# A decoder trunk on one core: operands of products begin at multiples of 128 bytes, and the written order of the pieces changes with it

## The chip, the core and the metric

The kernel runs on one core of a Trainium2 chip. TensorE (PE in the rows) multiplies, VectorE (DVE), ScalarE (ACT) and GpSimd (POOL) work on tiles, SyncE (SP) issues the transfers. Operands lie in SBUF, 128 partitions side by side; products come out in PSUM, in 8 banks of 512 float32 columns. The metric is the device time of one execution in microseconds (us); less is better.

## The reference, cut to what matters

256 tokens of width 1024 go through two layers in float32. Layer 0 is a recurrent block with a gated FFN, layer 1 an attention block of three branches with a gated FFN:

```
u = rmsnorm(h); z = u @ w_in                      # 1024 -> 2048
y = gelu(z[:1024]); x = causal_conv(z[1024:])     # 4 taps
r, i = sigmoid(per-head products of x)            # 8 heads of 128
h += (y * scan(a(r), b(r, i, x))) @ w_out
h += (silu(g) * up) @ w_out2                      # g, up = u @ w_in2, hidden 2816
k, v of three branches = rmsnorm(h) @ kv_w        # compressed, selected, window
h += (gated sum of 3 softmax attentions, 16 heads of 64, 4 key groups) @ w_o
h += (silu(g) * up) @ w_out2                      # hidden 2816
```

## The kernel before, in words

Every large product is made of three on TensorE: both operands are split into a high part (a copy rounded to the type fp32r) and a low part (the rest), and `mm3` adds high x high, high x low and low x high into the same PSUM bank (lines 340 to 342; `z_mm` does the same on line 411).

**The stream of weights.** `Weights` brings 192 weight tiles, in the order of `STREAM`, from memory into a ring of 4 `raw` tiles on SP's queue. `pieces` splits each: the first piece copies it to a `wh` tile (ACT, lines 137 or 144), the second subtracts to a `wl` tile (DVE or POOL, lines 193 and 198); there are 6 of each. Tiles in `WHOLE` (the weights of the compression) are multiplied as they lie in `raw`, so the ring's place is free only when TensorE has read them. All these tiles have `WT` columns.

**Four stages.** Stage A, the recurrent block: 16 products `z` of 24 matmuls of 256 columns, the convolution and gates and a scan (`lru`), then 96 matmuls of 512 columns in `a_proj` (`accf0o`). FFN 0 and FFN 1 (`ffn`): 11 chunks of 256 hidden columns; in chunks 1 to 10 `in_fm` has four weight tiles of 24 matmuls each (stationary: 128 columns of `wh` or `wl`; moving: 256 columns of the activation `u`), then `out_both` has two tiles of 12 matmuls (stationary: 128 columns of the hidden activation `fhh`, `fhl`; moving: 512 columns of `wh` or `wl`). Stage B, the attention: `kc_mm`, `q_mm` and `v_mm` (key, query and value products), `cm_mm` (the compression, 60 columns, straight from `raw`), `scores`, `tr_p`, `pv_mm`, `o_mm`.

**What sets the order.** In stages A and B the order of every engine is written by hand as the tables `PLAN_A` and `PLAN`: `play` runs one piece of a generator for each word (`z12` a product, `w14` a split's first or second piece, `l2` a piece of the scan, `cm02` a compression product); a letter behind it picks an engine (A, V, G) or a bank (a, m, t). In the FFNs, program order and free buffers set it.

**Where operands begin.** A tile of 1072 float32 columns has 4288 bytes a partition, 33.5 times 128, so of the 16 tiles raw, wh and wl, which lie behind each other, every second begins 64 bytes past a multiple of 128. The addresses in the built program, modulo 128, of the operands that this text speaks of:

| operand | before | after |
|---|---|---|
| raw, wh, wl | 64 and 0 in turn | 0 |
| activations u (moving in z and in_fm) | 64 | 0 |
| fhh, fhl in FFN 0 / in FFN 1 (stationary in out_both) | 96 / 64 | 0 / 0 |
| yh, yl (stationary in a_proj) | 32 | 0 |
| qT, kh, kl, vh, vl, identr, negr | 64 | 0 |
| msk (the identity of transposes), gw, zero | 32 | 0 |

By these addresses, before: product z1 has wh and wl at 0, z2 both at 64. In FFN 0, the four tiles of a chunk's `in_fm` have (wh, wl) at (0, 64), (64, 64), (64, 0), (0, 0); in FFN 1 at (64, 64), (0, 0), (0, 64), (64, 64). In the first half of the `out_both` of FFN 0 that begins at 190.69 us the moving wh and wl begin at 64, in its second half at 0.

Of the kernel before, what the change touches and what calls it, by code (L numbers as in the profile page):

```python
# [57 lines left out]
PLAN_A = """  # L58
na0aV na0 na1 na0 na0 na1 na1 nt0 na1t e0 nt0 w0 w0G e0 nt0 nt0 nt0 nt0 nt1a nt1m nt1 nt1a nt1t nt1 w1 w1 w2 w3 w2V z0
c0 d0 d0 d0 c0 d0 d0 d0 c0 d0 c0 w3G z1 d0G d0 d0 d0 d0 c1 c1 c1 c1 d0 d0 d0 z2 d0 d0 d0 w4 w4 g0 g0 g1 g1 g1 c2 d0 d0  # L60
g0 d0 c2 d0 d0 d0 c2 c2 w5 d0 d0 d0 d0 z3 c3 d0 d0 c3 d0 g2 g2 g2 d0 d0 c3 d0 d0 d0 c3 w6 w6 z4 g3 g3 w7 g3 c4 d0 d0
d0 c4 w5G d0 d0 d0 c4 d0 d0 d0 c4 w7 z5 g4 g4 g4 c5 d0 d0 d0 c5 c5 d0 d0 d0 d0 l0 l1 w8 w8G z6 d0 d0 c5 g5 g5 g5 d0 d0
d0 c6 c6 c6A d0 d0 d0 d0 l2t d0 c6 w9 z7 c7 w9a g6 g6 g6 d0 d0 d0 c7 d0 d0 d0 d0 d0 c7 d0 d0 w10 w11 w11G c7 l0 w10 z8
l1 g7 g7mA w12 w13 g7m l0V l0V l1 l3t l1 l1 l2a l0 z9 y0A z10 l2 l3a l3 w12G l2 y0V l3 w13G l2 l3 y1 y1V w14 y0 y0
w14a y2 y2V y1 y1 w15 w15 z11 y3 y2 y3V w16a w16 y2 z12 z13 y4 y4V y3 y3 y5 y5V w17 w17 z14 y4 y4 w18 w18 z15 y6 y6V
y5 y5 w19 gf0 w20 w19 y7 y7 o00 y6 y7 y6 y7 w20 o01 o02 o03 o10 o11 w21 w21 w22 w22 o04 o05 w23 w23 o12 w24 w24 o06
o07 r0 r0 r0 r0 r0 r0 o13 w25 w25 o14 o15 w26 w26 w27 w27V o16 nf0 nf0 nf0 nf0 nf0 nf0 o17 r1 r1 r1 r1 r1 r1a
"""


PLAN = """
w90 w91 w91 w92 hn0 w90 hn0 hn0G hn0 hn0A nt0 hn1 nt0 nt0 nt0 hn1 w92G kc00 kc01 nt0 nt0 hn1 w93V hn1 hn1 kc02 w93 nt1
nt1 w94V nt1 kc03 nt1 w94 kc10 nt1V kc04 w95V nt1 kc11 w95 kc12 w96V w97 w96 kc05 kc06 w97 x0 w98V w98 kc07 kc13 kp0
cp0 kp0 kc14 w99V kp0 w99 kc15 w100 ct011 ct011 kc16 ct000V kp0 kc17 ct000V ct010 kp0 ct010 kp0V q00 w100 kp1 w101G
kt00 kp1t kt00 w101 kp1 q01 q02 kt00 kp1 ct001 w102A q03 cp1 ct001 ct101 ct100 w103 w102 ct101 q10 q11 q12t w104A kt01
kp1 w103 w104 ct100 w105 bl0V q04 kt01V q05 bl0aV bl0V q06 bl0 kp1V w105 q07 ct110 qp00 qg0 qp01 qp00 qp00 q13V q14
ct110 q15 w106V qp00 qp00 qp00 qg0 w106 qp00 w107 qp01 qp01 w107 w108 qp01 qp01 qp01V w109 qp01 w108 qp02 qt000 q16
q17 qp10V qp02 qp02 qt000 cm00aA w109G qp02 qp02 w110 qt010 kt01 qp10 qp10 cm01 qt010m qg1 w110 qg1 qg1 w111 ct111
ct111 s000t w111 qp02 qg0G cm02G cm03 qp02 w112 bl1V v00 s000 bl1 s010m s010 qp11 s000 bl1 bl1 w113V qt011a w112 qt011
v01V qp11 qp11 s010 qp10 qp10 qp10 s011t cg0 qp10V kt10 v02 s011 qp12A s001 w113 kt10G qp11 qp11 cg0 w114m w114tG s000  # L80
s000 v10 cg0 v11 s001 s001 s010 v12 kt10 qp12 qp12 cg0 v03 cg0 w115 kt11a s010 s011 s020 w115G w116V v13 co0t qt021a
vp0V cm10m vp0 qt100V qt021V w117 kt11 kt11 co0 qt020m qp11 s020t ck w116G qp12V qp12 qp12V qt020 cm11 cm12 s020 ckA
qt100 s011 gG qp12 w117 ck ck s001 qt121a s001 cm13 vp1 vp1 s020 ck s021m cg1 qp11 ck ck qt120a s021m cg1 s011 t000m
qt120t qt121 s030t cg1 qt111a qt110 t000V cs00a s030V cs01 cs03 t000 s021 cg1 cs02A cg1 cz0t qt110 t010m t010 t001m
s020V s100 cz0V w118 s030 co1a co1V cz0 s100 cz0 cz0 qt111 cv cv s030 t010 s031 s030 cz0 s100 t011m s021 t001V cs10t
s031A cz0 cs12 cs11 t001 cs13 s021 cz0V s101 s100 cz0V s031 s100 t020a pt00m cv cz1 s110t s101 t011 s110 pt00 pt02a
s031G s102t s031 t011 s101 pv00a t020 s101 pt01m s102V t021m s101 t030a pt01 cz1 t031a t020 s102 s102 s103m pt02V s102
pv00V t021 pv01a s110 cz1 s103 cz1 s103 pt03 t021 pv02 s110 s110 pv00 pv01V pv00 s103 s111t cz1V pv00 cz1 s103 pt03
t030 pv01 pv01 s112 s111 t031 pv02 cz1 t030 s111 t100 t101m w118G pv02 s111 t100 t031 pv03a t103aA pv01 t102 cz1V t101
s112 w119a s122 s121m pv02 pv02 t101a s111 cz1 s113m t100 t103t t102 pt10 s112 t102 s120t w119G t103 pt10a pv03V s113V  # L90
pv10t s130 s112 pv03 pv03V pv03 s113 s112 s113 s113V s120 w120 s120 o00G w120 pv10 t110m w121 t113 s121 w121G o01
t110m s121 s120 s120V o02t t110 w122 s122 pt11m t112m pv10 pv10 pt11V t112 pv10 o03 t113 pt12 t112 s121 t111m t111
w122G s121 t113 s130 s131m s122 o04 t111 pt12V s130 s123t s123 s131 s123 pv11 s122 s122 s130 s130 s131 s123 s123V o10
pv11 w123 s131 pv11 pv11V t120 pv11 s131 t122 w123 t123m s132m t120 t120 t123V o11 t122 t122A w124 t121 t121V o12
s133t o05 s132 s132 w124G t123 s133 pt13m o13 s132 s132V w125 w125G s133 t121 pt13V pv12t s133 s133V w126 w127V x1
w127G pv12V t132V pv12 t131m pv12 t130m pv12 o06 t132V t132 t130 t130 w126G t133 t131 t131 o07 t133 t133 on0 on0 o14
pv13 w128V on0 on0 on0 o15 pv13 pv13 pv13 u pv13 w128 w129V u u o16 u u o17 u w129G on1 on1 on1 on1t on1aA
"""
# [1137 lines left out]
```

## Time and profile before

| | us |
|---|---|
| median of 3 runs (lowest to highest) | 649.74 (648.31 to 651.39) |
| profiled execution | 650.03 |
| its span, first to last instruction | 648.1 |
| PE busy | 627.9 |
| DVE busy | 412.0 |
| ACT busy | 325.8 |
| POOL busy | 118.1 |

The profiled execution is 0.3 us above the median, and 1.9 us of it lie outside the span. A matmul's busy time overlaps with the next one's, so what a matmul costs is read from the distance between starts, not from its busy time. [...]

### The profile page before, as it was taken

How to read it: one execution, taken by the hardware profiler on the slowest of the kernel's cores; microseconds unless marked ns; L12 is line 12 of the kernel's file. 1: busy time of each engine (PE TensorE's matmuls, PEld its weight loads, DVE VectorE, ACT ScalarE, POOL GpSimd, SP SyncE). 2: the span in 40 equal slices, each digit the busy share in tenths (PEclk: the TensorE clock that was granted, in tenths of full speed). 3: DMA queues.
4: the chain of work that ended last, by engine and by line, in shares of the span. 5: the costliest groups of instructions: out<-in, count | busy, mean ns of one | idle time of the engine just before them, and what ended most of it. 6: DMA issues, size and time to landing. Idle time of an engine off the chain costs nothing.

```text
span 648.1 us, 10441 instructions
## 1 busy us (share of the span) xinstructions
PE 627.9 (97%) x4067; PEld 560.7 (87%) x4067; DVE 412.0 (64%) x636; ACT 325.8 (50%) x595; POOL 118.1 (18%) x132
## 2 busy tenths in 40 slices
PE   7998899999999999999998999999999999999997
PEld 5898777999999999978998796776899999999996
DVE  5888957665555555469963878988765555555542
ACT  5579645454444444443624467855454444444430
POOL 3215020300000000001453547764100000000000
PEclk8999799999999999999996998999999999999999
DMA  8443654875555655526425140234285565556621
GB/s 294 137 163 131 193 196 135 282 250 196 179 185 190 194 189 183 184 94 206 153 83 192 66 163 1 98 99 130 92 272 191 193 194 173 191 192 192 191 70 66
DMA packets 31380, 106.68 MB, mean 165 GB/s; under 512 B 4014, under 2 KB 5730, under 8 KB 31203
## 3 DMA queue, kind: packets, MB, share of 16 engines
q1 hardware_dynamic: 31331, 106.02, 49.5%
q8 instruction: 32, 0.52, 0.3%
q14 instruction: 17, 0.14, 0.1%
HBM read 104.95 MB, written 1.05 MB: 164 GB/s over the span
## 4 chain that ended last, share of the span: by engine, by line
PE 86%; DVE 7%; ACT 4%; DMA 1%; issue 1%; POOL 0%; SPq 0%; DVEq 0%; ACTq 0%
PE accf L342 6%; PE accf L340 6%; PE accf L341 6%; PE f1u L342 3%; PE f1u L341 3%; PE f1u L340 3%; PE f0g L340 3%; PE f1g L340 3%; PE f0g L342 3%; PE f0g L341 3%; PE f1g L341 3%; PE f0u L341 3%; PE f1g L342 3%; PE f0u L340 3%; PE f0u L342 3%; PE z L411 3%
## 5 line engine op out<-in xcount | busy, mean ns | idle before, releaser
L198 DVE TENSOR_TENSOR wl<-raw,wh 128x1024 fp32r<-128x1024 f32 x147 | 180.1, 1230 | 146.5 <-ACT wh L137 146.3
L137 ACT CAST wh<-raw 128x1024 fp32r<-128x1024 f32 x161 | 167.9, 1049 | 184.5 <-issue 41.8
L342 PE MATMUL accf<-wh,fhl 128*128 128x512 f32 x176 | 69.5, 395 | 0.0
L340 PE MATMUL accf<-wh,fhh 128*128 128x512 f32 x176 | 69.4, 395 | 0.0
L341 PE MATMUL accf<-wl,fhh 128*128 128x512 f32 x176 | 69.2, 393 | 0.0
L198 POOL TENSOR_TENSOR wl<-raw,wh 128x1024 fp32r<-128x1024 f32 x17 | 42.6, 2512 | 46.4 <-ACT wh L137 32.1
L342 PE MATMUL f1u<-uhf,wl 128*128 128x256 f32 x160 | 45.1, 282 | 0.0
L341 PE MATMUL f1u<-ulf,wh 128*128 128x256 f32 x160 | 45.0, 281 | 0.0
L340 PE MATMUL f0g<-uhf,wh 128*128 128x256 f32 x160 | 45.0, 281 | 0.0
L340 PE MATMUL f1u<-uhf,wh 128*128 128x256 f32 x160 | 44.9, 281 | 0.0
L340 PE MATMUL f1g<-uhf,wh 128*128 128x256 f32 x160 | 44.8, 280 | 0.0
L340 PE MATMUL f0u<-uhf,wh 128*128 128x256 f32 x160 | 44.8, 280 | 0.0
L341 PE MATMUL f0u<-ulf,wh 128*128 128x256 f32 x160 | 44.7, 279 | 0.0
L341 PE MATMUL f1g<-ulf,wh 128*128 128x256 f32 x160 | 44.7, 279 | 0.0
L342 PE MATMUL f1g<-uhf,wl 128*128 128x256 f32 x160 | 44.6, 279 | 0.0
L342 PE MATMUL f0g<-uhf,wl 128*128 128x256 f32 x160 | 44.6, 279 | 0.0
L341 PE MATMUL f0g<-ulf,wh 128*128 128x256 f32 x160 | 44.6, 279 | 0.0
L342 PE MATMUL f0u<-uhf,wl 128*128 128x256 f32 x160 | 44.4, 277 | 0.0
L342 PEld LDWEIGHTS accf<-wh,fhl 128*128 128x128 f32 x176 | 33.1, 188 | 7.8
L341 PEld LDWEIGHTS accf<-wl,fhh 128*128 128x128 f32 x176 | 33.1, 188 | 7.0
L340 PEld LDWEIGHTS accf<-wh,fhh 128*128 128x128 f32 x176 | 33.1, 188 | 6.8
L1011 ACT ACTIVATE pr<-s,sm 128x128 f32<-128x128 f32 (+1 forms) x64 | 26.2, 422 | 8.9 <-DVE sm L1003 6.6
(310 smaller groups left out, 1525.9 us busy)
## 6 DMA issues: line engine op xcount, KB each, us to landing
raw<-in_wsrc_dram SPq DMA_DIRECT2D x184, 512.0 KB, 3.7
raw<-in_wsrc_dram SPq DMA_DIRECT2D x8, 536.0 KB, 4.2
hres<-in_x_dram SPq DMA_DIRECT2D x4, 256.0 KB, 3.3
gw<-in_gatew_dram SPq DMA_DIRECT2D x1, 1024.0 KB
gain<-in_gains_dram SPq DMA_DIRECT2D x2, 512.0 KB, 6.5
out_dram<-hres SPq DMA_DIRECT2D x8, 128.0 KB, 1.8
tab<-in_hvec_dram SPq DMA_DIRECT2D x1, 256.0 KB, 4.9
tab<-in_rope_c_dram SPq DMA_DIRECT2D x1, 128.0 KB, 3.8
```

Source lines behind the costliest of these rows:

```text
L137: self.nc.scalar.copy(dst, src)
L198: self.on.pick(nc.gpsimd if i in LOW_ON_POOL else nc.vector).tensor_tensor(lo[:, :w], t[:, :w], f32v(h[:, :w]), ALU.subtract)
L340: T.matmul(ps, ah, bh, start=start, stop=False)
L341: T.matmul(ps, ah, bl, start=False, stop=False)
L342: T.matmul(ps, al, bh, start=False, stop=stop)
L411: T.matmul(zs[i], w[:, k * P:(k + 1) * P], u[:, k, :], start=(n == 0 and k == 0), stop=(n == 2 and k == KT - 1))
L1011: A.activation(pr[:, h1 + i, br], sv[:, br], AF.Exp, bias=sm[:, 0, h0 + i, br:br + 1], accum_out=sm[:, 1, h0 + i, br:br + 1])
```

## The change

`WT` becomes 1088 columns (4352 bytes, 34 times 128), the query tile gets 16 columns of zeros behind the gate columns (so `QC` begins its second and third product at columns 320 and 704; the first is 320 columns wide instead of 304, and 8 transfers are 544 KB instead of 536), small tiles are padded to multiples of 32 columns, and two small tiles of `cmp_k` share the places of two of `cmp_gelu`. Both tables are written anew with the same pieces; here is one row of `PLAN_A` before and after.

```
-    + [1024] * 8 + [1072] * 8 + [1024] * 12 + [1024] * 8
+    + [1024] * 8 + [1088] * 8 + [1024] * 12 + [1024] * 8
...
-WT = 1072
+WT = 1088
...
-l1 g7 g7mA w12 w13 g7m l0V l0V l1 l3t l1 l1 l2a l0 z9 y0A z10 l2 l3a l3 w12G l2 y0V l3 w13G l2 l3 y1 y1V w14 y0 y0
+w11 w11G c7 c7 l0 l1 z8G g7 g7mA w12 w13m w10 g7m w12G l0V l1 l3tA l1 w14 l1 w13V l0V l0G l2a l3a l3m z9 y1m y1V y1 l2
...
-    msk = const.tile([P, 128 + 32 + 2], F32, name="msk")
+    msk = const.tile([P, 192], F32, name="msk")[:, 0:162]
-    hb = pa.tile([P, 16], F32, name="hb")
+    hb = pa.tile([P, 32], F32, name="hb")[:, 0:16]
-    bgate = p1.tile([P, 48], F32, name="bgate")
+    bgate = p1.tile([P, 64], F32, name="bgate")[:, 0:48]
...
-    QC = ((0, 304), (304, 688), (688, 1072))
+    QC = ((0, 320), (320, 704), (704, 1088))
...
-        tmp = pt1.tile([60, 1, HD], F32, name="kctmp")
+        tmp = pt1.tile([60, 128], F32, tag="hx0", name="kctmp", bufs=1)[:, None, 0:HD]
...
-            sms[t, g] = p3.tile([P, 3, HG, 2], F32, tag="sm", name=f"sm{t}{g}", bufs=4)
+            sms[t, g] = p3.tile([P, 3, HG, 2], F32, tag="sm", name=f"sm{t}{g}", bufs=5)
...
-    rows(np.concatenate([bw[:, 0:256], bw[:, D:], bw[:, 256:D]], 1), 1)
+    rows(np.concatenate([bw[:, 0:256], bw[:, D:], np.zeros((D, 16), np.float32), bw[:, 256:D]], 1), 1)
```

The two FFNs have the same order on TensorE as before. Two places of the plans matter below. The first is TensorE in stage B, from the first compression product (`cm`) to the first value product (`v`). Before:

```order
L868 MATMUL cm_3521<-bf_3363,raw_3308 128x60 x8
L844 MATMUL qtp_3536<-identr,qs_3423 128x128 x4
L868 MATMUL cm_3521<-bf_3363,raw_3353 128x60 x8
L750 MATMUL ctp_3569<-msk,cs_3294 64x128 x2
L993 MATMUL s_3574<-kh,qTh 128x256
...
L868 MATMUL cm_3521<-bf_3363,raw_3356 128x60 x8
L868 MATMUL cm_3521<-bf_3363,raw_3402 128x60 x8
L340 MATMUL v_3612<-wh_3532,uhkv 128x512
```

And now:

```order
L871 MATMUL cm_3529<-bf_3382,raw_3340 128x60 x8
L847 MATMUL qtp_3538<-identr,qs_3457 128x128 x4
L871 MATMUL cm_3529<-bf_3382,raw_3365 128x60 x8
L753 MATMUL ctp_3555<-msk,cs_3291 64x128 x2
L871 MATMUL cm_3529<-bf_3382,raw_3377 128x60 x8
L996 MATMUL s_3586<-kh,qTh 128x256
...
L871 MATMUL cm_3529<-bf_3382,raw_3404 128x60 x8
L343 MATMUL v_3615<-wh_3560,uhkv 128x512
```

The first score product `s` stands behind the third compression product instead of ahead of it. On ACT, which makes the copy of the queries (`qTh`) that `s` reads and the high part of the next value tile (L144, now L147), the order at this place was:

```order
L137 CAST qTh<-qtp_3487 128x512
L144 ACTIVATE wh_3532<-raw_3460,vec 128x512 x2
L137 CAST qTh<-qtp_3536 128x512
L833 ACTIVATE gate_2967<-gate_2967 128x48
L144 ACTIVATE wh_3565<-raw_3467,vec 128x512 x2
```

And it is now:

```order
L140 CAST qTh<-qtp_3538 128x512
L836 ACTIVATE gate_2967<-gate_2967 128x48
L140 COPY T_2970<-ctp_3555 64x2x128 x2
L147 ACTIVATE wh_3560<-raw_3459,vec 128x512 x2
L147 ACTIVATE wh_3578<-raw_3472,vec 128x512 x2
```

The copy of the queries stands ahead of the weight copy that needs a fresh transfer into the ring. The other place is ACT in stage A, between the gates and the copy of weight tile 14, which product z14 reads (`wh_675` before, `wh_601` now). Before:

```order
L433 ACTIVATE TH<-tr_583,sp 128x256
L443 ACT_TABLE_LOAD
L443 ACTIVATE TH<-TH 128x512
L455 ACT_TABLE_LOAD
L455 ACTIVATE yg_629<-z_554 128x256
L443 ACT_TABLE_LOAD
L443 ACTIVATE TH<-TH 128x512
L455 ACT_TABLE_LOAD
L455 ACTIVATE yg_672<-z_604 128x256
L137 CAST wh_675<-raw_547 128x1024
```

And now:

```order
L436 ACTIVATE TH<-tr_582,sp 128x256
L140 CAST wh_601<-raw_546 128x1024
L446 ACT_TABLE_LOAD
L446 ACTIVATE TH<-TH 128x512 x2
L458 ACT_TABLE_LOAD
L458 ACTIVATE yg_640<-z_615 128x256
```

The copy moved ahead of the square roots, and two square roots now follow each other, so two table loads are gone (8 in the program instead of 10). On DVE the subtraction of tile 13 (`w13V`) came from POOL.

## Rows read from the trace of the kernel before

**Rows 1.** Page, part 4: the chain that ended last, by engine.
```profile
PE 86%; DVE 7%; ACT 4%; DMA 1%; issue 1%; POOL 0%; SPq 0%; DVEq 0%; ACTq 0%
```

**Rows 2.** Stages A, FFN 0, B, FFN 1: busy us, granted clock, DMA.
```profile
core 0: us, PE busy (x) PEld busy (x) DVE busy (x) ACT busy (x) POOL busy (x), PEclk, DMA share, GB/s
0.00:97.00 97.00, 86.44 (x535) 76.88 (x536) 74.19 (x120) 65.30 (x106) 25.23 (x22) 0.95 0.55 186
97.00:285.00 188.00, 187.58 (x1294) 172.66 (x1293) 104.12 (x124) 87.12 (x122) 7.51 (x19) 1.00 0.58 192
285.00:462.00 177.00, 171.50 (x976) 142.11 (x975) 138.05 (x278) 94.59 (x259) 85.34 (x92) 0.95 0.36 118
462.00:648.00 186.00, 182.36 (x1268) 169.09 (x1266) 95.65 (x117) 78.79 (x108) 0.00 (x0) 1.00 0.52 170
```

**Rows 3.** Timeline, PE, stage A: z1, z2 and what follows (start, busy).
```profile
16.99 1.07 PE L411 MATMUL z<-uha,wh 128*128 128x256 f32 x8
...
19.71 1.12 PE L411 MATMUL z<-uha,wh 128*128 128x256 f32 x8
...
22.57 1.02 PE L426 MATMUL gt<-X,gw 128*128 128x256 f32 x4
```

**Rows 4.** Timeline, PE, FFN 1: one chunk, from tile to tile.
```profile
487.40 0.28 PE L340 MATMUL f1g<-uhf,wh 128*128 128x256 f32 x1
...
490.26 0.28 PE L340 MATMUL f1g<-uhf,wh 128*128 128x256 f32 x1
...
492.99 0.28 PE L340 MATMUL f1u<-uhf,wh 128*128 128x256 f32 x1
...
498.67 0.39 PE L340 MATMUL accf<-wh,fhh 128*128 128x512 f32 x1
...
504.21 0.28 PE L340 MATMUL f1g<-uhf,wh 128*128 128x256 f32 x1
```

**Rows 5.** Timeline, PE, FFN 0: one chunk and its output products.
```profile
179.52 0.28 PE L340 MATMUL f0g<-uhf,wh 128*128 128x256 f32 x1
...
190.69 0.39 PE L340 MATMUL accf<-wh,fhh 128*128 128x512 f32 x1
...
193.49 0.39 PE L340 MATMUL accf<-wh,fhh 128*128 128x512 f32 x1
...
196.29 0.28 PE L340 MATMUL f0g<-uhf,wh 128*128 128x256 f32 x1
```

**Rows 6.** Page, part 5: the split's subtraction on DVE (busy us, mean ns).
```profile
L198 DVE TENSOR_TENSOR wl<-raw,wh 128x1024 fp32r<-128x1024 f32 x147 | 180.1, 1230 | 146.5 <-ACT wh L137 146.3
```

**Rows 7.** Stretches with a lowered clock, and a full one (columns as Rows 2).
```profile
60.00:70.00 10.00, 5.41 (x39) 5.00 (x38) 9.93 (x16) 7.85 (x12) 0.37 (x1) 0.86 0.22 63
344.00:357.00 13.00, 12.50 (x53) 11.92 (x54) 4.85 (x12) 6.16 (x18) 3.49 (x7) 0.50 0.57 190
360.00:420.00 60.00, 57.46 (x369) 45.89 (x368) 48.39 (x122) 39.64 (x133) 37.76 (x49) 0.97 0.25 87
```

**Rows 8.** Timeline, PE, stage B: value products at the lowered clock.
```profile
353.20 0.63 PE L341 MATMUL v<-wl,uhkv 128*128 128x512 f32 x1
...
354.91 0.63 PE L342 MATMUL v<-wh,ulkv 128*128 128x512 f32 x1
```

**Rows 9.** The chain in stage B, in order of time (start, us).
```profile
339.11 3.51 DMA raw<-in_wsrc_dram
342.65 1.33 ACT wh L144 x2
...
346.15 6.71 PE cm L868 x32
...
374.27 3.59 PE cm L868 x32
```

**Rows 10.** Timeline, ACT and DVE, stage A: before product z14.
```profile
61.93 1.28 ACT L455 ACT_TABLE_LOAD   x1
```

**Rows 11.** Waits of PE.
```profile
PE z L411 <- DVE wl L198: 2.8, 1, 2.8
```

More of the change, by code (lines that the diff above doesn't have):

```diff
@@ L58 @@
 PLAN_A = """
[L59 to L63, printed above, removed]
@@ L64 @@
-l1 g7 g7mA w12 w13 g7m l0V l0V l1 l3t l1 l1 l2a l0 z9 y0A z10 l2 l3a l3 w12G l2 y0V l3 w13G l2 l3 y1 y1V w14 y0 y0
-w14a y2 y2V y1 y1 w15 w15 z11 y3 y2 y3V w16a w16 y2 z12 z13 y4 y4V y3 y3 y5 y5V w17 w17 z14 y4 y4 w18 w18 z15 y6 y6V
-y5 y5 w19 gf0 w20 w19 y7 y7 o00 y6 y7 y6 y7 w20 o01 o02 o03 o10 o11 w21 w21 w22 w22 o04 o05 w23 w23 o12 w24 w24 o06
-o07 r0 r0 r0 r0 r0 r0 o13 w25 w25 o14 o15 w26 w26 w27 w27V o16 nf0 nf0 nf0 nf0 nf0 nf0 o17 r1 r1 r1 r1 r1 r1a
+na0tA na0G na0 na0 nt0A na1 na1 e0t nt0 na1G na1t nt0 nt0tV nt0 w0A nt1a nt1G nt1 nt1a nt0a e0 nt1t nt1 w1 w1 w2 w3
@@ L68 @@
+y1 y0A y0mV z10 y2V w14a y0 l2 y0t z11 y3a l2 y3V w15 w15 y2V w16aA l3t l3G w17 y2 y2 w16 z12 z13 y4 y4V y3 y3 y5 y5V
+z14 w17 y4 y4a w18 w18 z15 y6 y6V y5 w19 w20 w19 gf0 y7 y7 y5 w20 o00 o01V o02 o03 o10 o11 w21 w22 w21 w22 o04 w23 o05
+y6 y7 y7 y6 o06 w23V o07 r0 r0 r0 r0 o12 w24 w24 r0 r0 w25 w25 o13 o14 o15 w26 w26 w27 o16 nf0 nf0 nf0G nf0 nf0 nf0
+o17 r1 r1 r1 w27V r1A r1 r1aV
 """
 PLAN = """
-w90 w91 w91 w92 hn0 w90 hn0 hn0G hn0 hn0A nt0 hn1 nt0 nt0 nt0 hn1 w92G kc00 kc01 nt0 nt0 hn1 w93V hn1 hn1 kc02 w93 nt1
@@ L73 @@
[L73 to L97, printed above, removed]
+w90 w90 w91 w91 hn0 hn0 hn0G w92 hn0 hn0A nt0 nt0 hn1 nt0a nt0 kc00 hn1 w92G nt0 hn1 kc01G w93 hn1G hn1 nt0 w93 kc02
@@ new lines @@
+s121 pt11m pv10 pv10 pt11V t112 o03 pt12 t113 t112 w122G t111m t111 s121 t113 s131m s122 o04 t111 pt12V s130 s123t
+s123 s123 s131 s131 s123 pv11 s123V s122 s122a s130 s130 pv11 s131 w123 pv11 pv11V pv11 o10 t120 s131 t122 w123 t123m
+s132m t120 t120 t123V t123 o11 t122 t122A w124 w124G t121 t121V o12 s133t s132 o13 s133 s132 s132 s132V t121 w125
+w125G s133 pt13m pt13V s133 s133V w126 o05 w127V x1A w127G pv12t pv12V t132V pv12 t131m pv12 t130m o06 t132V t133 t130
+pv12 t130 w126G t132 t131m t131 o07 t133 t133 on0 on0 o14 w128V pv13 on0 on0 on0 o15 pv13 pv13 pv13 uA w128 w129V u
@@ L98 @@
+pv13 u u o16 o17V u uG w129G on1 on1 on1 on1t on1aA
 """
@@ L236, in hybrid_trunk @@
     W = Weights(nc, on, wpool, wsrc, 4, 6)
-    warm = const.tile([P, 1], F32, name="warm")
+    warm = const.tile([P, 32], F32, name="warm")[:, 0:1]
     V.memset(warm, 0.0)
@@ L252, in hybrid_trunk @@
             nc.sync.dma_start(grow[0:1, :], gains[0:1, :])
-    msk = const.tile([P, 128 + 32 + 2], F32, name="msk")
+    msk = const.tile([P, 192], F32, name="msk")[:, 0:162]
     nc.sync.dma_start(msk, masks[:, 0:162])
-    vec = const.tile([P, 80], F32, name="vec")
+    vec = const.tile([P, 96], F32, name="vec")[:, 0:80]
     nc.sync.dma_start(vec, vecs)
@@ L272, in hybrid_trunk @@
     vcmp = msk[:, 160:162]
-    mhalf = const.tile([P, 16], F32, name="mhalf")
+    mhalf = const.tile([P, 32], F32, name="mhalf")[:, 0:16]
     GP.memset(mhalf, -0.5)
@@ L348, in hybrid_trunk @@
     uah, ual = u_tiles("a")
-    hb = pa.tile([P, 16], F32, name="hb")
+    hb = pa.tile([P, 32], F32, name="hb")[:, 0:16]
     sp = pa.tile([P, 8, 8], F32, name="sp")
-    euler = pa.tile([P, 8], F32, name="euler")
+    euler = pa.tile([P, 32], F32, name="euler")[:, 0:8]
     gw = pa.tile([P, 16, P], F32, name="gw")
@@ L628, in hybrid_trunk @@
     b2 = pt1.tile([60, 2, HD], F32, name="b2")
-    b1v = pt1.tile([P, 4], F32, name="b1v")
-    bgate = p1.tile([P, 48], F32, name="bgate")
+    b1v = pt1.tile([P, 32], F32, name="b1v")[:, 0:4]
+    bgate = p1.tile([P, 64], F32, name="bgate")[:, 0:48]
     selt = pt1.tile([60, G, 64], F32, name="selt")
@@ L871, in cmp_gelu @@
     def cmp_gelu(kv):
-        hx, h2, h3 = (pt1.tile([P, 2, 60], F32, tag=f"hx{i}", name=f"hx{kv}{i}", bufs=1) for i in range(3))
+        hx, h2, h3 = (pt1.tile([P, 128], F32, tag=f"hx{i}", name=f"hx{kv}{i}", bufs=1)[:, 0:120].rearrange("p (u c) -> p u c", u=2) for i in range(3))
         for u in range(2):
@@ L895, in cmp_k @@
     def cmp_k():
-        tmp = pt1.tile([60, 1, HD], F32, name="kctmp")
-        st = pt1.tile([60, 2, 1], F32, name="kcst")
+        tmp = pt1.tile([60, 128], F32, tag="hx0", name="kctmp", bufs=1)[:, None, 0:HD]
+        st = pt1.tile([60, 32], F32, name="kcst")[:, 0:2].rearrange("p (a b) -> p a b", b=1)
         yield from head_rms(kc[:, None, :], st, tmp, 1, 60)
         V.tensor_scalar(kc, kc, st[:, 1, 0:1], None, ALU.mult)
-        kcd = pt1.tile([60, 2, HD], F32, name="kcd")
+        kcd = pt1.tile([60, 2, HD], F32, tag="hx1", name="kcd", bufs=1)
         V.tensor_tensor(tmp[:, 0, 0:32], kc[:, 32:64], ctab[:, 1, 0:32], ALU.mult)
@@ L996, in scores @@
         yield
+        if pair not in pp:
+            pp[pair] = p3.tile([P, 4 // nk, 2, nk, P], F32, tag="pr", name=f"pr{t}{g}{b}", bufs=3)
         if (t, g) not in sms:
-            sms[t, g] = p3.tile([P, 3, HG, 2], F32, tag="sm", name=f"sm{t}{g}", bufs=4)
+            sms[t, g] = p3.tile([P, 3, HG, 2], F32, tag="sm", name=f"sm{t}{g}", bufs=5)
         sm = sms[t, g]
@@ L1004, in scores @@
         yield
-        if pair not in pp:
-            pp[pair] = p3.tile([P, 4 // nk, 2, nk, P], F32, tag="pr", name=f"pr{t}{g}{b}", bufs=3)
         pr = pp[pair]
```

24 lines of the change are left out of this document (added).

## The prediction

> **What bounds the kernel now.** I read the chain of waits first: 86% of the span is TensorE's own work [rows 1]. Then the windows by stage [rows 2]: in FFN 0 PE is busy 187.58 of 188 us and in FFN 1 182.36 of 186, at the full clock (1.00, 2.4 GHz); DVE, ACT and the transfers have much room there (DVE 104.12 and 95.65, ACT 87.12 and 78.79, DMA share 0.58 and 0.52). So in 374 of 648 us the time is the number of matmuls times the distance of one start from the next, and anything that shortens this distance is paid out in full. Stages A and B are mixed: PE is nearly always at work, but DVE is at 74.19 of 97 and 138.05 of 177, and the granted clock averages 0.95, so there are stretches at half clock.
>
> Then I looked for what sets the distance, since busy times overlap. The cleanest pair is z1 and z2 [rows 3]: the same 24 matmuls of 256 columns, the same moving tiles, PE without a gap. z1, whose weight tiles begin at multiples of 128, takes 19.71 - 16.99 = 2.72 us, 113.3 ns a matmul; z2, whose weight tiles begin 64 bytes past one, takes 22.57 - 19.71 = 2.86 us, 119.2 ns. FFN 1 repeats it [rows 4]: the first tile of the chunk (wh, wl both at 64) takes 490.26 - 487.40 = 2.86 us, the second (both at 0) 2.73 us. Stationary operands off the multiple thus cost about 5.5 ns a matmul. For 512 columns no aligned pair exists. With the stationary operand at 96, FFN 0 needs (196.29 - 190.69)/24 = 233.3 ns, equally in its first half, where the moving operand begins at 64, and in its second, where it begins at 0: 2.80 us each [rows 5]. With it at 64, FFN 1 needs (504.21 - 498.67)/24 = 230.8 ns [rows 4]. So the stationary start is what shows; the moving start alone does not.
>
> **The change part by part. 1, the alignment in the FFNs.** A chunk's 96 matmuls of 256 columns take 190.69 - 179.52 = 11.17 us in FFN 0 [rows 5] and 498.67 - 487.40 = 11.27 us in FFN 1 [rows 4]. At z1's 113.3 ns they take 10.88: 0.29 and 0.39 us less. For the 24 of 512 columns I take twice the aligned 256, 226.7 ns, as the nearest row: 5.44 us instead of 5.60 and 5.54, so 0.16 and 0.10 less. Ten chunks of the first kind and eleven of the second give 10 x 0.29 + 11 x 0.16 = 4.7 us in FFN 0 and 10 x 0.39 + 11 x 0.10 = 5.0 us in FFN 1; the 48 matmuls of 512 columns of each first chunk add some 0.25 each. **Sum 10.2 us.** Bounds: below, only the tiles now wholly or partly off the multiple in 256 columns gain and 512 stays, 6.8 us; above, the distances of the half clock, see rival 1. What lies beside: the weights must come faster by 2.7%. With DVE at 55%, ACT at 46% and the transfers at 58% of FFN 0 that is free.
>
> **2, the alignment in stage A.** Eight of 16 z have tiles at 64: 8 x 24 x 5.9 ns = 1.1 us; the 96 matmuls of a_proj, whose stationary operand is at 32, taken like FFN 0's, give 96 x 6.6 ns = 0.6. But from 60 to 70 us DVE is busy 9.93 of 10 [rows 7], so what PE saves there it waits. **I take 1.0** of 0 to 1.7.
>
> **3, the alignment in stage B.** 10.2 of 374 us is 2.7%; on the whole 177 us that would be 4.8. Transposes, compression products and waits have no such share. **I take 1.5** of 0 to 4.8. The first query product grows from 304 to 320 columns, 48 matmuls of 16 columns more: 48 x 16 x 0.44 ns (113.3/256) = 0.3 us; it is inside this term, as are the 8 KB more in 8 transfers.
>
> **4, the new order in stage A.** Product z14 waits for its weights, 2.8 us in one wait for the subtraction [rows 11], and behind it the clock falls (0.86 in the mean of 60 to 70). The new order copies weight 14 ahead of the square roots and saves two table loads of 1.28 us [rows 10] on ACT. But DVE was full, and it gets one subtraction of 1.23 us [rows 6] that POOL did. z14 may start some 2 us sooner, then a_proj waits on the next subtractions, which now end late behind it. At best the wait and the clock's share, about 5 us; at worst nothing. **I take 1.5.**
>
> **5, the new order in stage B.** This is the largest hole in PE's work. The weight copy for the value product waited for a transfer that could start only when the first compression product had freed its place in the ring: 339.11 + 3.51, then ACT until 343.98 [rows 9]; the copy of the queries stood behind it on ACT, the scores behind that on PE, and the compression products behind the scores, at 346.15. After the gap the clock is 0.50 from 344 to 357 [rows 7], so 32 matmuls of the compression take 6.71 us where they later take 3.59 [rows 9], and a 512-column product (354.91 - 353.20)/4 = 427 ns [rows 8]. Now neither the copy of the queries nor the third compression product stands behind the weight copy, so the latter can start at about 341.5, four to five us earlier, and the places for the next two value tiles come free that much earlier too. With the clock kept up, another 3.1 us. Bound above: 8. What is late next is DVE: from 360 to 420 it is busy 48.39 of 60 [rows 7], in order, and can take up only a part. Bound below: 0, if the stall reappears at the value product. **I take 3.5.** The shared small tiles of cmp_k cost nothing: their next writer stands behind the last reader on the same engine.
>
> **Sum.** 10.2 + 1.0 + 1.5 + 1.5 + 3.5 = 17.7 us from the profiled 650.03, which is 0.3 above the median: **632 us**.
>
> **Rivals.** *1, more than the sum: with both operands aligned the stream runs at its column rate.* No row has a 256-column product with both starts at 0, so it can't be excluded. At half clock 512 columns take 427 ns, which is 213.5 at full clock, and 256 would take 107. A chunk would take 96 x 0.107 + 24 x 0.2135 = 15.4 us instead of 16.8; 1.4 x 21 = 29 us in the FFNs, some 5 in A and B and 3 to 5 from the order: 612 to 616. Against it: the moving start made no difference in rows 5. [...] Chance 0.10.
>
> *2, the alignment does nothing.* The 113 against 119 would then come from something that goes with the buffer, say which half of a PSUM bank is written, as tile 2 of a chunk writes the other half than tile 1. Against it: z1 and z2 write the same columns. Then only parts 4 and 5 count: 645. [...] Chance 0.07.
>
> *3, the order gives nothing, or takes back.* Only parts 1 to 3 are left, or up to 8 us are lost to new waits: 637 to 645. Chance 0.23.
>
> *4, slower: the clock.* A gap on PE in stage A's a_proj (each weight tile waits for a full DVE) or at B's value products lets the clock fall, as from 344 to 357. In 13 us of dense products half the work is lost, 6.5 us. Against 12.7 us from parts 1 to 3 it decides with the third new stretch: 650 - 12.7 + 3 x 6.5 = 657. Two such stretches stood in stages A and B before; three more than that is far. Chance 0.05.
>
> **How the numbers follow.** The forecast has 0.55 and its own range is 626 to 637. For 8 in 10 the range takes in most of rival 3 and leaves out rivals 1, 2 and 4: 621 to 643. A difference under 0.5% (3.2 us) is about what the runs cannot tell from no change. Under 646.5 lie the forecast, rivals 1 and 3 and part of 2: 0.89; within 0.5% the rest of 2 and a milder 4: 0.06; slower 0.05.
>
> **What would show it.** Part 1: in both FFNs every tile of 24 takes 2.72 us, and a chunk 16.3 instead of 16.8; FFN 0 and FFN 1 each about 5 us shorter. [...] Part 4: z14 waits less and a_proj starts before 75 us. Part 5: no wait of the scores for the copy of the queries, and PEclk near 1.0 over the compression products; 32 of these in 3.6 us. Wrong would be: FFN chunks unchanged, or DVE's queue in stage B ending no earlier than now.

## The result, and the profile after

The changed kernel takes **638.84 us** (median of 4 runs, 638.22 to 639.63) against 649.70 (648.31 to 651.39) before: 0.9832 of it, with a 95% interval of 0.9807 to 0.9858. The forecast was 632, in a range of 621 to 643. The sign and the range held, but the reason did not: aligned operands made the FFNs' products slower on balance, and the whole gain, and more, came from the order.

The first view is the windows of the kernel after, by its own four stages and then for the two stretches that were at a lowered clock before (columns as in [rows 2]; PEclk is the granted TensorE clock as a share of the full one):

```profile
0.00:97.00 97.00, 88.90 (x552) 77.50 (x553) 77.48 (x126) 64.01 (x107) 22.88 (x22) 0.98 0.56 193
97.00:280.00 183.00, 182.81 (x1264) 170.71 (x1263) 100.12 (x117) 84.90 (x120) 7.66 (x17) 1.00 0.58 194
280.00:457.00 177.00, 175.15 (x1036) 146.02 (x1035) 141.71 (x280) 104.88 (x274) 87.24 (x94) 1.00 0.37 122
457.00:637.00 180.00, 175.99 (x1221) 164.00 (x1219) 88.96 (x108) 72.88 (x100) 0.00 (x0) 1.00 0.54 172
60.00:70.00 10.00, 8.75 (x70) 8.26 (x69) 9.93 (x18) 5.76 (x12) 0.00 (x0) 1.00 0.30 105
344.00:357.00 13.00, 12.82 (x79) 11.09 (x78) 11.25 (x26) 9.51 (x37) 11.82 (x17) 1.00 0.74 250
```

The clock is at 1.00 over both stretches. Such fixed windows do not say where a stage ends, so I take the last transposes ahead of FFN 0, the first ahead of stage B and the last ahead of FFN 1 as landmarks. In the timeline of PE before they were

```profile
104.72 1.12 PE L328 MATMUL ntpf<-msk,xnf 128*128 128x128 f32 x8
...
285.90 1.27 PE L328 MATMUL ntpkv<-msk,xnkv 128*128 128x128 f32 x8
...
462.92 1.04 PE L328 MATMUL ntpf<-msk,xnf 128*128 128x128 f32 x8
```

and after they are

```profile
100.85 1.29 PE L331 MATMUL ntpf<-msk,xnf 128*128 128x128 f32 x8 [0.16 <-DVE xnf L323]
...
283.79 1.04 PE L331 MATMUL ntpkv<-msk,xnkv 128*128 128x128 f32 x8
...
448.81 1.03 PE L331 MATMUL ntpf<-msk,xnf 128*128 128x128 f32 x8
```

Stage A is 3.9 us shorter. FFN 0 is longer, 182.9 us for 181.2. Stage B is 12.0 us shorter (165.0 for 177.0). FFN 1, to the end of the span, is longer, 187.9 for 185.2. The sum is 11.4, the difference of the spans 648.1 and 636.7.

Why the FFNs lost shows in the timeline of PE after, one chunk of FFN 0 as in [rows 5], from tile to tile:

```profile
142.50 0.28 PE L343 MATMUL f0g<-uhf,wh 128*128 128x256 f32 x1
...
145.38 0.28 PE L343 MATMUL f0g<-uhf,wh 128*128 128x256 f32 x1
...
148.26 0.28 PE L343 MATMUL f0u<-uhf,wh 128*128 128x256 f32 x1
...
151.14 0.28 PE L343 MATMUL f0u<-uhf,wh 128*128 128x256 f32 x1
...
154.02 0.40 PE L343 MATMUL accf<-wh,fhh 128*128 128x512 f32 x1
...
159.49 0.28 PE L343 MATMUL f0g<-uhf,wh 128*128 128x256 f32 x1
```

Each tile of 24 takes 2.88 us, 120.0 ns a matmul, where 2.72 was forecast and 2.72 to 2.86 had been seen; the 24 of 512 columns take 5.47 us instead of 5.60. The chunk needs 16.99 us, 0.2 more than before. In FFN 1 the tiles take 2.88 us as well, and the 24 of 512 columns, whose `fhh` begins at 128 modulo 256 where FFN 0's begins at 0, take 5.58 us instead of 5.54. z1, the aligned tile that the forecast was built on, also goes at (18.88 - 16.00)/24 = 120.0 ns now:

```profile
16.00 1.12 PE L414 MATMUL z<-uha,wh 128*128 128x256 f32 x8
...
18.88 1.12 PE L414 MATMUL z<-uha,wh 128*128 128x256 f32 x8
```

What the order won shows in the windows of the three half-clock stretches of before (columns as in [rows 2]):

```profile
67.00:74.00 7.00, 5.44 (x25) 5.44 (x26) 7.00 (x13) 6.41 (x12) 0.00 (x0) 0.51 0.56 175
343.00:358.00 15.00, 13.50 (x56) 12.77 (x57) 6.45 (x14) 7.95 (x24) 3.49 (x7) 0.54 0.55 175
391.00:395.00 4.00, 4.00 (x22) 3.49 (x22) 3.63 (x8) 2.62 (x11) 2.54 (x3) 0.57 0.00 0
```

The clock withheld there is 7 x 0.49 + 15 x 0.46 + 4 x 0.43 = 3.4 + 6.9 + 1.7 = 12.0 us. After, none of the three stretches is left. The first two stand in runs 1 and 11 below too, which have the old order; the third is missing from the trace of run 1, so the order cannot be credited with its 1.7 us. The chain of waits after, in stage B, shows what became of the stall of [rows 9]:

```profile
339.12 1.75 PE cm L871 x16
340.88 4.03 DMA raw<-in_wsrc_dram
344.94 1.34 ACT wh L147 x2
...
348.69 0.23 PE v L343
...
361.92 5.37 PE cm L871 x48
```

The transfer and the weight copy behind it still take 5.4 us, but they no longer stop TensorE: it works 12.82 of the 13 us from 344 to 357, on scores, value products and compression products that now stand elsewhere in the order, and 48 compression products take 5.37 us (3.6 for 32) where 32 took 6.71. In stage A, z14's wait of [rows 11] is gone from the waits of PE, and two small ones for weights stand in `a_proj`:

```profile
PE accf0o L344 <- DVE wl L201: 1.7, 2, 1.2
```

### The profile page after: what moved, and what is told of

It reads as the page before. It is cut to its first block, busy times and chain, and to the rows that moved or that the text cites. A ratio compares the mean times of both kernels' runs of the same rounds, so it can differ in the third digit from the quotient of the medians.

```text
span 636.7 us, 10442 instructions
## 1 busy us (share of the span) xinstructions
PE 622.8 (98%) x4067; PEld 558.2 (88%) x4067; DVE 408.3 (64%) x630; ACT 326.7 (51%) x598; POOL 117.8 (18%) x133
## 4 chain that ended last, share of the span: by engine, by line
PE 84%; DVE 7%; DMA 3%; ACT 3%; issue 2%; POOL 1%; SPq 0%; DVEq 0%; ACTq 0%
PE accf L344 6%; PE accf L343 6%; PE accf L345 6%; DMA raw<-in_wsrc_dram 3%; PE f1u L343 3%; PE f0g L345 3%; PE f1u L344 3%; PE f0u L344 3%; PE f1g L343 3%; PE f0u L343 3%; PE f0u L345 3%; PE f1u L345 3%; PE f0g L344 3%; PE f1g L345 3%; PE f0g L343 3%; PE f1g L344 3%
## 5 line engine op out<-in xcount | busy, mean ns | idle before, releaser
L201 POOL TENSOR_TENSOR wl<-raw,wh 128x1024 fp32r<-128x1024 f32 x16 | 40.1, 2513 | 43.2 <-ACT wh L140 29.4
```

The costliest lines, as they stand in the source:

```text
L201: self.on.pick(nc.gpsimd if i in LOW_ON_POOL else nc.vector).tensor_tensor(lo[:, :w], t[:, :w], f32v(h[:, :w]), ALU.subtract)
```

## The experiments

Starts of operands are given modulo 256 from here on, read from the addresses in the built programs. Distances are worked out from the starts in the traces.

**1 and 2: the two halves of the change apart.** The first kernel is the changed one with both tables of before, the second the kernel before with both new tables.

```
 # aligned, old order (from the kernel after)
-PLAN_A, PLAN = the new tables
+PLAN_A, PLAN = the tables of before
 # old starts, new order (from the kernel after)
-WT = 1088
+WT = 1072
...                     (and every pad)
```

> The changed kernel with the two order tables of before: the alignment alone. Theory A (the order made the gain, the alignment costs: equal starts of the two operands modulo 128 make a 256-column matmul 120 ns): the FFN chunks stay at 16.98 and 17.09 us, the half-clock stretches of stages A and B come back, 650 to 656 us, not faster than before. Theory B (the alignment helps in stages A and B, the order little): 638 to 643.

> The kernel before with the two new order tables: the order alone. Theory A: the FFN chunks stay at 16.77 and 16.81 us, stages A and B are shorter by some 16 us as in the changed kernel, 632 to 636 us, so faster than the changed kernel. Theory B: 645 to 650.

Measured: aligned with the old order 652.86 us (652.04 to 653.88; 1.0065 of before, 1.0044 to 1.0086). Old starts with the new order 634.68 (633.42 to 639.54; 0.9798, 0.9756 to 0.9841). So alignment alone costs about 4 us and the order alone gives about 14.6; the two add up to the result. The tables were swapped whole, so no run says which of the moves in them is worth how much. In the aligned kernel with the old order, z1 takes 2.88 us too, and the clock from 344 to 357 is low again; its windows:

```profile
344.00:357.00 13.00, 10.63 (x45) 10.05 (x46) 5.32 (x11) 7.51 (x20) 3.50 (x7) 0.61 0.63 194
```

Two things in run 2's trace were not expected. The order in which the splits run decides which `wh` tile meets which `wl` tile, so the new order changed the pairs of starts although the tiles lie where they lay: a chunk takes 17.00 us in FFN 0 and 16.74 in FFN 1, not 16.77 and 16.81. Over ten chunks each that costs some 1.6 us, so in stages A and B the order gave more than the 14.6. And its traced execution, of 639.54 us, has a half-clock stretch in stage B that the traces of before and after lack:

```profile
375.00:386.00 11.00, 10.44 (x48) 9.82 (x49) 7.11 (x17) 6.58 (x24) 5.85 (x11) 0.54 0.00 0
```

It withheld 11 x 0.46 = 5.1 us and begins right behind two waits of PE, 0.51 us for ACT and 0.61 us for DVE. The kernel after has the same two waits (0.50 and 0.61) at the full clock. The other three executions of run 2, 633.42 to 634.75 us, have a mean granted clock of 0.997 to 1.000 against 0.992. So the new order removed the two stretches that it was written against, but it still has a place where the clock falls in some executions.

**3: u at 64.** The changed kernel with 16 columns more ahead of u, so that u begins at 64 and the weights stay at 0. The tiles behind u move with it: `fhh` and `fhl` then begin at 64 in FFN 0 and at 192 in FFN 1.

```
-        g = work.tile([P, D], F32, tag="gain", name=f"gain{i}", bufs=1)
+        g = work.tile([P, D + 16], F32, tag="gain", name=f"gain{i}", bufs=1)
```

> The changed kernel with the activations u (and the tiles behind them on that side) shifted by 64 bytes, the weights left at multiples of 256. Theory A (what costs is the same start modulo 128 in both operands): all 256-column matmuls take 113.3 ns, a chunk of FFN 0 takes 16.3 us instead of 16.98, the whole 622 to 627 us. Theory C (aligned starts are as fast as they get, 120 ns has another cause, such as the distance of 4352 bytes between the weight tiles): 120 ns stay, 638 to 640.

Measured: 635.49 us (633.88 to 640.29; 0.9809, 0.9765 to 0.9853). The median is over 3 us below the changed kernel's, but the two intervals overlap; what shows it is the trace. A chunk takes 16.91 us in FFN 0 and 16.81 in FFN 1, where the changed kernel needs 16.99 and 17.09, some 3.6 us less over ten chunks each. Moving one operand off the multiple made the products faster, so it is not alignment that counts. But the tiles did not reach 113.3 ns, and neither theory's time came; in the timeline of PE in FFN 0 a tile takes 152.61 - 149.78 = 2.83 us, 117.9 ns:

```profile
149.78 0.28 PE L343 MATMUL f0u<-uhf,wh 128*128 128x256 f32 x1
...
152.61 0.39 PE L343 MATMUL accf<-wh,fhh 128*128 128x512 f32 x1
```

The traced execution, of 640.29 us, has the half-clock stretch of run 2's trace too, from 375 to 386 us.

**4: distances by themselves.** A kernel without the reference's work: groups of 24 matmuls, ordered as in a weight tile, with chosen starts.

```
+group(256, so, mo)  # mo: start of the moving operand, so: of the stationary one
```

> A kernel that leaves out all work of the reference (it copies x to the output) and runs groups of 24 matmuls like those of the FFN, of 256, 512 and 384 columns, each group with its own start of the stationary and of the moving operand modulo 256. Theory A (the relative start): 256 columns take 120 ns where both starts are equal modulo 128 and 113.3 where they are 64 apart, whichever of the two is the shifted one. Theory D (absolute: the stationary must be at 0 and the moving at 64): with moving 0 and stationary 64 they take 119 to 120, and only moving 64 with stationary 0 or 128 takes 113.3. 512 columns: A has no figure; the rows so far lie between 226 and 234.

Measured, on its timeline of PE (`pma` is moving at 0; the stationary operand begins at 0 in `sa`, 48 in `sd`, 64 in `se`, 96 in `sg`):

```profile
24.59 0.28 PE L80 MATMUL pmasa<-mh,sh 128*128 128x256 f32 x1
27.46 0.28 PE L80 MATMUL pmasb<-mh,sh 128*128 128x256 f32 x1
...
33.14 0.28 PE L80 MATMUL pmasd<-mh,sh 128*128 128x256 f32 x1
35.97 0.28 PE L80 MATMUL pmase<-mh,sh 128*128 128x256 f32 x1
38.69 0.28 PE L80 MATMUL pmasg<-mh,sh 128*128 128x256 f32 x1
```

Equal starts need 2.87 us for 24, 48 bytes apart 2.83, 64 apart 2.72 (113.3 ns each). Moving at 64 with stationary at 64 was as slow, 120.0, as both at 0; moving 0 with stationary 64 and moving 64 with stationary 0 both gave 113.3. So theory D is out: no absolute start decides. But theory A does not hold as it was written either. Four other pairs that are 64 apart modulo 256 (moving 0 with stationary 192, 64 with 128, 128 with 64, 128 with 192) took some 117.8 ns, and starts 128 apart took 118.4 to 118.5, not 120. For 512 columns equal starts were the best, 226.7. Groups of 384 columns took 173.1 to 176.9.

**5: a map.** The same groups for every pair in steps of 64 bytes, modulo 512.

```
+for mo in range(8):
+    for so in range(8):
+        group(n, 64 * so, 64 * mo)
+for mo in range(8, 16, 2):             # and 256 columns once more
+    for so in range(8):
+        group(256, 64 * so, 64 * mo)
```

> The reference's work is left out (x is copied to the output); what is left is groups of 24 matmuls as in a weight tile (high x high, high x low, low x high), one after the other, for every pair of starts of the moving and the stationary operand in steps of 64 bytes, modulo 512, with 256 and with 512 columns; both parts of an operand have the same start. Theory A, the relative start modulo 256 alone counts: each distance repeats along a diagonal of the map, 113.3 ns where the stationary operand begins 64 bytes ahead of or behind the moving one, 117.8 to 118.4 for 128, 120.0 for equal starts; 512 columns 226.7 for equal starts and 229 to 233 elsewhere. Theory B, the addresses themselves count: pairs of the same difference have different distances, and moving 64 with stationary 0 gives 117.8, as in the kernel with u at 64, while 64 bytes and 256 more of both give 113.3, as in the first map.

Measured, ns from start to start in the second half of each group. The distances repeat with 256 bytes; this is the corner, with the moving start down and the stationary one across:

```
256 columns    0      64     128    192      512 columns    0      64     128    192
  0          120.0  117.8  118.3  117.8        0          226.7  233.3  231.7  228.9
 64          117.8  120.3  113.3  118.4       64          228.9  226.7  233.3  231.7
128          118.8  117.8  120.0  117.8      128          232.8  228.9  226.7  233.3
192          117.8  118.2  117.8  120.0      192          233.3  231.7  228.9  226.7
```

For 512 columns the relative start modulo 256 is nearly all: equal 226.7, stationary ahead by 64 bytes 233.3, by 128 231.7 to 232.8 (233.6 at one pair of run 4), by 192 228.9. For 256 columns equal is the slowest, 120.0, and 128 apart gives 118.2 to 118.8. A distance of 64 has two values: stationary ahead by 64 gave 113.3 in the rows of 64 and 320 and 117.8 in the six others, and 64 behind gave 117.8 here and 113.3 in the map before. So theory A holds but for this pair. The last loop shows that no address explains its two values: there the stationary operand ahead by 64 gave 113.3 with moving at 640 and 896, whose starts modulo 512, 128 and 384, had given 117.8.

**6: u at 192**, with weights at 0, so that the stationary operand is ahead by 64.

```
-        g = work.tile([P, D + 16], F32, tag="gain", name=f"gain{i}", bufs=1)
+        g = work.tile([P, D + 48], F32, tag="gain", name=f"gain{i}", bufs=1)
```

> The kernel after with u at 192 bytes past a multiple of 256 instead of at 64, weights as they are at multiples of 256. Theory A, it is the relative start, and the better side is the one that the kernel before had (moving at 192, stationary at 0: 113.4 ns): all products of 256 columns go at 113.3 ns, a chunk of an FFN takes 10.88 + 24 x 0.231 = 16.4 us instead of 16.9, and the time falls some 10 us below that of u at 64, to 625 to 627. Theory B, moving operands at odd multiples of 64 all give what u at 64 gave, 117.8 ns: 635.

Measured: 629.07 us (628.50 to 629.68; 0.9693, 0.9670 to 0.9715). In FFN 0 the four tiles of a chunk take 10.91 us, near 113.3 ns a matmul. In FFN 1 the chunks alternate, as its timeline of PE shows:

```profile
484.07 0.28 PE L343 MATMUL f1g<-uhf,wh 128*128 128x256 f32 x1
...
494.97 0.39 PE L343 MATMUL accf<-wh,fhh 128*128 128x512 f32 x1
...
500.56 0.28 PE L343 MATMUL f1g<-uhf,wh 128*128 128x256 f32 x1
...
511.87 0.39 PE L343 MATMUL accf<-wh,fhh 128*128 128x512 f32 x1
```

The four tiles of one chunk take 494.97 - 484.07 = 10.90 us, those of the next 511.87 - 500.56 = 11.31, with the same starts in both. That is why 629 came and not 626. Between runs 3 and 6 the hidden activations moved too (here to 192 in FFN 0 and 64 in FFN 1), so these two runs alone do not show that the side of u decides; in run 9 below u lies at 192 and every tile goes at 117.8.

**7: the new order in stage B alone**, on the kernel before.

```
 PLAN_A = the table of before
-PLAN = the table of before
+PLAN = the new table
```

> The kernel before with the new order in stage B alone; stage A's order and all starts of operands as before. Theory A, the gain of the order is nearly all stage B's (11.9 us of the landmarks, from the wait for the transfer and the half-clock stretches behind it): 638 to 640. Theory C, stage A's order gives its 4.2 us and B the rest: 649.5 - 15 + 4 = 638 to 639 as well, and stage A then ends at 104.9 on its landmark as before; if stage A's order gives nothing by itself and its 4.2 us come from the clock, stage A ends near 101 here.

Measured: 639.78 us (638.47 to 640.27; 0.9855, 0.9834 to 0.9876), 9.0 us less than before. Beside run 2 (0.9798) this leaves (0.9855 - 0.9798) x 649 = 3.7 us for stage A's order; by the two intervals it can be anything from nothing to some 7. The landmark of stage A agrees with 3.7: it stands at 102.98 us in run 7's trace and at 99.58 in run 2's. It was expected at 104.9 or near 101 here and lies between them; 1.7 us of its distance to before are a half-clock stretch near 12 to 16 us that the trace of before has and run 7's has not. Run 7 keeps stage A's half-clock stretch, 0.89 in the mean of 60 to 75 us, and has none from 330 to 400.

**8: what makes the distance.** Groups with fewer columns in the stationary operand, so that its load reads less, and pairs of groups to see whether the first decides the second's value. The reference's work is left out again.

```
+for cols in (128, 96, 64, 32):
+    group(n, so, 0, cols=cols)          # so: 0, 64, 128, 192
+group(n, ro, 0, count=24)  # 24, 23 or 22, then
+group(256, 64, 0)
```

> The reference's work is left out (x is copied to the output). First part: groups of 24 matmuls of 256 and of 512 columns, moving at 0, stationary at 0, 64, 128 and 192 modulo 256, with stationary operands of 128, 96, 64 and 32 columns. Theory A, the load of the next stationary operand and the read of the moving one hinder each other in SBUF: the fewer columns the stationary operand has, the smaller the difference between the starts, and the distance nears some 107 ns (213.5 for 512) with 32 columns. Theory B, the starts matter by themselves (a matmul begins late for its operand's start): the same differences, 113 to 120 and 226.7 to 233.3 ns, with any number of columns. Second part: groups of 256 columns with the stationary operand 64 bytes ahead or behind, each after a group of another kind with 24, 23 or 22 matmuls; if the state left by the group before decides between the 113.3 and the 117.8 ns seen so far, the same pair shows both values, by the group ahead of it.

Measured, on its timeline of PE (each name covers four groups, 96 matmuls, with the four starts):

```profile
26.57 0.28 PE L81 MATMUL w256c128s<-mh,sh 128*128 128x256 f32 x1
...
37.95 0.28 PE L81 MATMUL w256c96s<-mh,sh 128*96 128x256 f32 x1
...
60.20 0.28 PE L81 MATMUL w256c32s<-mh,sh 128*32 128x256 f32 x1
...
71.08 0.40 PE L81 MATMUL w512c128s<-mh,sh 128*128 128x512 f32 x1
...
162.56 0.28 PE L81 MATMUL y64n256r0k<-mh,sh 128*128 128x256 f32 x1
...
165.39 0.28 PE L81 MATMUL x256r0k<-mh,sh 128*128 128x256 f32 x1
...
184.85 0.28 PE L81 MATMUL y64n256r128k<-mh,sh 128*128 128x256 f32 x1
...
187.59 0.28 PE L81 MATMUL x256r128k<-mh,sh 128*128 128x256 f32 x1
```

With 128 columns in the stationary operand 256-column matmuls take 11.38/96 = 118.5 ns in the mean of the four starts; with 32 they take 10.88/96 = 113.3, and 113.3 at each of the four. With 96 columns the four starts still lie between 116.2 and 120.0, with 64 three of them take 113.3 and the one 128 apart 116.7. So the differences shrink with the columns of the stationary operand, as in theory A, for 256 columns. That the two reads meet in SBUF is not shown by this; fewer stationary columns also mean fewer rows of the product. The floor is 113.3, not 107. For 512 columns neither theory holds: with 32 columns the four starts gave 229.8 to 231.7, so the spread shrinks, but the good value of equal starts, 226.7, is lost as well.

The last four rows are two groups with the same starts (stationary ahead by 64): 24 matmuls in 165.39 - 162.56 = 2.83 us behind a group of equal starts, and 24 in 187.59 - 184.85 = 2.74 behind a group of 23 that is 128 apart (113.3 in its second half); behind 24 of that kind it was 117.8. So what ran ahead decides between 117.8 and 113.3 for the next group, and the value then holds through the group. Each combination ran once. The pair with the stationary operand 64 behind has both values too, 113.3 behind equal starts and 117.8 behind starts 128 apart. Behind 512-column groups of equal starts all three counts gave 117.8; behind those with the stationary operand ahead by 192, 113.3, 113.3 and 117.8.

**9 and 10: the products ahead.** From u at 192, with a pad ahead of `fhh` and `fhl`: at 0 in both FFNs (they were at 192 in FFN 0 and at 64 in FFN 1), or at 192 in both.

```
         pf = fp.enter_context(tc.tile_pool(name=f"pf{layer}", bufs=1))
+        pf.tile([P, 48 if layer else 16], F32, name=f"fpad{layer}")     # at 0
 ...
+        if layer:
+            pf.tile([P, 32], F32, name="fpad1")                         # at 192
```

> The kernel with u at 192, and the hidden activations fhh and fhl (stationary in the products of 512 columns) at 0 modulo 256 in both FFNs, as their moving weights. By the map the 512-column products go at 226.7 ns instead of 228.9 in FFN 0 and 233.3 in FFN 1, 0.6 and 1.7 us less. Theory A, each product's distance is that of its own pair: nothing else changes, 626.8. Theory B, the state in which the 512-column products leave TensorE decides between 113.3 and 117.8 ns for the 256-column products behind them: FFN 1's chunks, every second of which now goes at 117.8, go all one way, down to 624.5 or up to 629 in the whole.

> The kernel with u at 192, with fhh and fhl at 192 modulo 256 in FFN 1 as they are in FFN 0. Theory A: 512 columns at 228.9 instead of 233.3 ns in FFN 1, 1.2 us less, 627.9, and every second chunk still at 117.8. Theory B: FFN 1 goes like FFN 0, all chunks at 113.3, another 5 x 96 x 4.5 ns = 2.2 us less: 625.7.

Measured: at 0, 633.21 us (631.17 to 636.59; 0.9756, 0.9720 to 0.9792); at 192, **625.73** (624.58 to 629.97; 0.9648, 0.9610 to 0.9685). With the hidden activations at 0, their own products reach the map's best value, as FFN 1's timeline of PE shows:

```profile
485.99 0.28 PE L343 MATMUL f1g<-uhf,wh 128*128 128x256 f32 x1
...
497.30 0.39 PE L343 MATMUL accf<-wh,fhh 128*128 128x512 f32 x1
...
502.74 0.28 PE L343 MATMUL f1g<-uhf,wh 128*128 128x256 f32 x1
```

5.44 us, 226.7 ns each; but every 256-column tile behind them goes at 117.8, and the chunk's four take 11.31 us. With 192 the 24 take some 0.05 us more, and the 256-column tiles take the better value, 2.72 us or 113.3 ns a matmul; the same timeline of that kernel:

```profile
491.79 0.28 PE L343 MATMUL f1u<-uhf,wh 128*128 128x256 f32 x1
...
494.51 0.39 PE L343 MATMUL accf<-wh,fhh 128*128 128x512 f32 x1
...
500.00 0.28 PE L343 MATMUL f1g<-uhf,wh 128*128 128x256 f32 x1
```

Theory B holds in its mechanism: the products ahead select the value. Its time for run 10, 625.7, came. Run 9's 633.21 lies above all that was expected, since that counted FFN 1 alone: in FFN 0, too, the four tiles went from 10.91 us to 11.31, some 3.5 us over ten chunks. Optimizing each product by its own pair thus lost some 4 us. Run 10 is the best version of this study, 13 us under the changed kernel.

**11: u at 192 with the old order.**

```
 # from u at 192
-PLAN_A, PLAN = the new tables
+PLAN_A, PLAN = the tables of before
```

> The aligned tiles with u at 192, but both tables of the order as in the kernel before: what alignment alone is worth with the better relative start. From the aligned kernel with the old order, 652.9, the 9.8 us that u at 192 gave with the new order are taken off: 643; if the gain hides behind the waits of stages A and B, some 2 us less: 645. By the theory of the prediction (starts at multiples of 128 are what counts) u at 192 could give nothing: 653.

Measured: 644.29 us (643.17 to 645.85; 0.9929, 0.9904 to 0.9955), 15.2 above the same starts with the new order. The windows show the withheld clock again:

```profile
60.00:75.00 15.00, 10.14 (x60) 9.52 (x59) 14.93 (x27) 11.67 (x21) 0.00 (x0) 0.77 0.48 159
330.00:380.00 50.00, 46.13 (x302) 42.59 (x301) 31.63 (x83) 22.73 (x81) 23.54 (x32) 0.86 0.44 137
```

Starts and order add up: the new order gave 14.0 us with everything aligned, 14.6 with the old starts and 15.2 with u at 192.

## Why the prediction was right in sign and wrong in cause

**The failed step** is "So the stationary start is what shows; the moving start alone does not." z1 and z2 differ in the stationary operand's start modulo 128, as the text said. But u, the moving operand, began at 192 in both: z1's weights at 0 and 128 were 64 away from it on either side, z2's at 64 and 192 were 128 away or equal. What I took for aligned against not aligned was 64 apart against 0 or 128 apart, and the pair could not tell the two readings apart, since u never moved. The change put u on the same start as the weights, the slowest case of the map: 120.0 ns where the forecast had 113.3. The pattern of [rows 4] fits too: its fast tile has weights at 0 modulo 128 beside a u at 64 modulo 128. The two halves of [rows 5], on which the second clause rested, are 512-column products, which follow other values; they could say nothing of 256 columns.

**Part 1** (10.2 us from the FFNs) came out as a loss: +1.8 and +2.7 us on the landmarks, as 256-column tiles went to 120.0 ns. Its term for 512 columns was right where the starts became equal: 5.47 us a chunk in FFN 0 against 5.44 forecast; in FFN 1, where they did not, it is 5.58. **Parts 2 and 3** (1.0 and 1.5) were not measured by themselves but rest on the same step; with part 1 they were to give 12.7, and run 1 gave minus 3.6.

**Part 4** took 1.5 of 0 to 5; some 3.7 was measured. The wait went, the clock stayed up and `a_proj` starts at 68.2 us instead of 75.7; DVE, full as before (9.93 of 10 us), made `a_proj` wait 1.7 us in two pieces, as was feared, but that did not lower the clock (1.00 in the mean of 68 to 96 us).

**Part 5** had the mechanism: the copy of the queries no longer behind the weight copy, the scores not behind it, the clock near 1.0 over the compression products, 32 of these in 3.6 us. Its size was off: 3.5 was taken, with 8 as the bound, and run 7 gave 9.0. The cost of the lowered clock had been read from 32 matmuls (3.1 us), not from the whole stretch, which withheld 6.9. That a full DVE would take up a part was a reason for the low figure; by the traces stage B became 12.0 us shorter, so it cannot have taken up much.

**The sum** missed by 6.8 us: alignment fell short by some 16 to 17 and the order exceeded its 5.0 by nearly 10. The number held by two errors that nearly cancelled, which is luck. None of its terms uses the 2.4 GHz that the prediction sets beside the full clock. The traces give the clock as a share only; as an estimate, the 427 ns for 512 columns at 0.50 of [rows 8] make 1.2 columns a ns there and 2.4 at the full clock; at 1.00 the best 512-column products took 226.7 ns (run 9), 2.26 columns a ns.

**The rivals.** Rival 1 (the column rate) did not occur: the lowest distance of 256 columns in any run is 113.3 ns, that of z1, and of 512 columns 226.7. Its time, 612 to 616, is by its own terms 611 to 613. Rival 2 had the alignment at nothing; the starts do matter, but the reason given, that z1 and z2 write the same columns, excluded only one confounder, the half of the bank, and not u's own start. Rival 3 (the order gives nothing) was the reverse of what happened. Rival 4 did not come in the kernel after: no new half-clock stretch stands in stages A and B of its trace. The traces of runs 2 and 3 hold one such stretch, where the rival had three. The case that occurred, aligned operands being the slower ones, was among none of them.

**Open.** What the state is that one group hands to the next (113.3 or 117.8 ns with the same starts) was not found; the runs show only that it exists, that the number of matmuls ahead can change it and that in this kernel, with u at 192, the start of the hidden activations selects it. Which moves of the new order keep the clock up, and why it still falls near 375 us in some executions, was not tested. Why 512 columns prefer equal starts (226.7 ns), and keep a spread when the stationary operand is small (229.8 to 231.7 with 32 columns), is open as well.

## What to carry to other kernels

Where two readings of a clean pair differ only in something that stayed fixed in the pair (here the moving operand's start), a few groups of matmuls with that one thing moved settle it before a rule is built on it. In a kernel like this one, back-to-back fp32r products are to be placed by the relative start of moving and stationary operand modulo 256 (256 columns: 120.0 ns with equal starts, 113.3 or 117.8 with starts 64 apart), with the products that alternate with them, and by a measured chunk rather than by each product's best. And a half-clock stretch is to be costed over its whole length from the granted clock: here the two that went with the old order withheld 10.3 us, and the new order gave 14.6.
